# An encoder trunk on one core: a second bias tile requested with the first, two PSUM banks for transposed probabilities, and sums of weight halves formed one split ahead

## The chip, the core and the metric

The kernel runs on one core of one Trainium2 chip. A core has five engines that run side by side, each strictly in the order of its own instruction list, and that wait for each other through semaphores: PE (TensorE, matrix products; PEld is its loading of weights), DVE (VectorE), ACT (ScalarE), POOL (GpSimd) and SP, which here only issues DMAs. [...] The metric is the device time of one execution in microseconds (us). Three runs of the kernel before took 2218.95, 2216.13 and 2218.43 us; the median is 2218.43 us.

## The reference

One inference step of a two-layer encoder trunk for 1024 prompt frames and 32 sample frames, all in float32. Layer 0 is an mLSTM mixer and a SwiGLU feed-forward block, layer 1 a sliding-window attention with 16 heads and a feed-forward block. Cut to what the change touches:

```python
def swiglu(x, w_gu, w_down):
    g, u = jnp.split(x @ w_gu, 2, axis=-1)
    return (jax.nn.silu(g) * u) @ w_down

def sink_attention(q, k, v, sinks, bias):
    s = jnp.einsum('bcqhgd,bckhd->bchgqk', q, k).astype(F32) * (HEAD_DIM ** -0.5) + bias
    sk = sinks.astype(F32).reshape(N_KV_HEADS, GROUP)[:, :, None, None]
    mx = jnp.maximum(jnp.max(s, -1, keepdims=True), sk)
    p = jnp.exp(s - mx)
    p = p / (jnp.sum(p, -1, keepdims=True) + jnp.exp(sk - mx))
    return jnp.einsum('bchgqk,bckhd->bcqhgd', p.astype(v.dtype), v)
```

## The kernel before

**Products.** Every float32 operand is split into a high part and a rest, and each product is three matmuls (L368 to L370: high by high, high by rest, rest by high). A weight comes from memory as a raw tile `wr` (L162, issued by SP), ACT copies its high part to `wh` (L208), and POOL, for some weights DVE, subtracts to get the rest `wl` (L210). One call of `_next` is one such split of one factor. Four raw tiles and five pairs of `wh` and `wl` rotate. A split is written into the program when a factor's last matmul has been written (`done`, L234), up to four factors ahead of its use.

**The up projection of the feed-forward block** runs over 22 tiles of hidden features in each layer. The first two are computed plainly; the other 20 take a fast 2 by 2 scheme with seven products in place of eight. A pair of raw tiles a and b (halves a1, a2, b1, b2) gives seven factors in the order a1, a2, b2, s2, s1, s3, s4. The last four are sums and differences, which DVE forms inside the raw tiles (`_source`: L176, L179, L180, L182): s1 = b1 + b2, s2 = s1 - a1, s3 = a1 - b1, s4 = a2 - s2. Each of these DVE instructions is written right before the ACT copy that reads it, or one or two copies before. The 24 matmuls of one factor take about 2.9 us, one tile about 20.4 us. Bank group A holds the sums that ACT copies out (L1362, L1372, L1379, and L1390 with the silu) before PE adds the next factor on top; group B holds products that DVE adds (L1367, L1375, L1382, L1383). Beside it, `stage` writes activations of earlier tiles to memory for the down projection: ACT (L1288), DVE or POOL (L1289), then a DMA (`hs_t`, `hs_x`). The down projection has pairs of the same kind.

**Attention** (from L1569) runs as a pipeline of five stages over pairs (j, b) of a two-head group and a block of 128 frames: `scores` (PE into two banks `psS`, then DVE adds the bias and takes the extreme, L1725), `soft` (ACT exponent L1737, DVE reciprocal L1741, POOL scaling L1743), `turn` (PE transposes the probabilities into bank `T`, L1763; ACT L1766 and DVE L1767 split them), `values` (PE into one of two banks `O`, L1778 and L1779) and `place` (L1787, L1789). A generator yields after each stage, and the stages are so written in between the matmuls of the query projections (`q_group`) and later of the first quarter of the output projection (L1218); the result of each projection lies in a rotating bank `d` until ACT and DVE have read it (L1623 and L1624, or L1221). `dense_psum(3)` gives `d` three banks here; `psS` has two, `O` two and `T` one, eight in all. The order on each engine is fixed when the program is built.

**The bias** of a head group is a tile `bt` (256 KB) with a smaller `sb` for the sample; two of each rotate. `load_bias` (L1649) has SP issue both DMAs and POOL fill the last column with the sinks. The first is requested at L1659, ahead of the attention's projections; each later one is requested when the first `scores` of the group before it is written (L1712).

## Time and profile before

| what | us |
|---|---|
| median of three runs | 2218.43 |
| the profiled execution: its own time | 2219.82 |
| the profiled execution: span from first to last instruction | 2218.0 |
| PE busy in the span | 2178.0 (98%) |
| DVE busy | 1468.7 (66%) |
| POOL busy | 1020.5 (46%) |
| ACT busy | 1002.6 (45%) |

Times within the execution are counted from the first instruction. Layer 0's fast up tiles run from about 521 to 930 us, its down projection to about 1168, attention from there to about 1430, and layer 1's feed-forward block to the end. A row of the timeline gives start, length, engine, source line, instruction, tile written and tiles read; a bracket at its end gives how long the engine stood idle before it and what ended that. A row of waits gives the waiting instruction, what released it, the total in us, the number of waits and the longest.

### The profile page before, as it was taken

What the parts mean: (1) busy time and instruction counts of PE and PEld (TensorE: products, weight loads), DVE (VectorE), ACT (ScalarE), POOL (GpSimd) and SP (SyncE); (2) the same over time, 40 slices, a digit from 0 to 9 for tenths busy, and PEclk for the clock granted to TensorE, in tenths of its full rate; (3) what the DMA queues carried; (4) which work ended last, traced back from release to release, by engine and by line L of the source; (5) the groups of instructions that cost most, each with busy time, mean ns of one, the idle gap of its engine ahead of it and who ended that gap; (6) DMA issues with size and microseconds to landing.
All of it is one profiled execution on the core that took longest, in us unless ns stands there. A gap on an engine that the chain in (4) does not pass through costs nothing.

```text
span 2218.0 us, 44293 instructions
## 1 busy us (share of the span) xinstructions
PE 2178.0 (98%) x17086; PEld 2149.8 (97%) x17086; DVE 1468.7 (66%) x2848; ACT 1002.6 (45%) x2259; POOL 1020.5 (46%) x982
## 2 busy tenths in 40 slices
PE   9999999999999999999998999999999999999997
PEld 9999999999999999999998999899999999999997
DVE  4465677787666665566667678888576666466657
ACT  4443455464344444321245778756444444422125
POOL 2544210004666566544525776600576666554441
PEclk9999999999999999999999999999999999999999
DMA  5221212212443343797515333521244434397712
GB/s 169 78 62 57 57 39 86 89 39 80 153 155 136 137 155 136 248 333 230 175 57 173 108 100 97 155 63 39 103 162 163 135 138 155 129 343 258 243 59 79
DMA packets 174500, 298.10 MB, mean 134 GB/s; under 512 B 18065, under 2 KB 130761, under 8 KB 174289
## 3 DMA queue, kind: packets, MB, share of 16 engines
q1 hardware_dynamic: 169936, 290.94, 39.9%
q10 hardware_dynamic: 4352, 4.33, 0.6%
q8 instruction: 135, 2.21, 0.4%
q14 instruction: 77, 0.62, 0.1%
HBM read 201.80 MB, written 82.94 MB: 128 GB/s over the span
## 4 chain that ended last, share of the span: by engine, by line
PE 61%; DVE 5%; ACT 3%; DMA 2%; issue 2%; POOL 2%; SPq 0%; POOLq 0%; DVEq 0%; ACTq 0%
PE A L368 9%; PE A L370 9%; PE A L369 9%; PE B L368 6%; PE B L369 6%; PE B L370 6%; PE d L368 4%; PE d L370 4%; PE d L369 4%; PE T L1763 1%; POOL s L1743 1%; DMA hs_x<-z 1%; DMA sx<-hs_t 1%; ACT act L471 1%; PE O L1778 1%
## 5 line engine op out<-in xcount | busy, mean ns | idle before, releaser
L210 POOL TENSOR_TENSOR wl_s<-wr,wh_s 128x512 fp32r<-128x512 f32 x224 | 316.6, 1433 | 262.6 <-ACT wh_s L208 187.6
L210 POOL TENSOR_TENSOR wl_a<-wr,wh_a 128x512 fp32r<-128x512 f32 x112 | 168.7, 1513 | 386.7 <-ACT wh_a L208 264.5
L368 PE MATMUL d<-sx,wh 128*128 128x264 f32 (+2 forms) x1068 | 341.3, 320 | 2.1 <-ACT wh L208 1.6
L370 PE MATMUL d<-sx,wl 128*128 128x264 f32 (+2 forms) x1068 | 325.7, 305 | 2.8 <-POOL wl L210 2.8
L369 PE MATMUL d<-sx,wh 128*128 128x264 f32 (+2 forms) x1068 | 324.8, 304 | 0.4 <-DVE sx L399 0.4
L208 ACT CAST wh_s<-wr 128x512 fp32r<-128x512 f32 x224 | 136.0, 619 | 323.4 <-DVE wr L180 295.6
L368 PE MATMUL A<-sx,wh_s 128*128 128x264 f32 x896 | 254.8, 284 | 1.8 <-ACT z L1372 1.8
L369 PE MATMUL A<-sx,wh_s 128*128 128x264 f32 x896 | 254.2, 284 | 0.0
L370 PE MATMUL A<-sx,wl_s 128*128 128x264 f32 x896 | 254.0, 284 | 0.0
L368 PEld LDWEIGHTS d<-sx,wh 128*128 128x128 f32 x1068 | 201.9, 189 | 5.8 <-ACT wh L208 2.3
L370 PEld LDWEIGHTS d<-sx,wl 128*128 128x128 f32 x1068 | 201.3, 189 | 4.2 <-POOL wl L210 3.9
L369 PEld LDWEIGHTS d<-sx,wh 128*128 128x128 f32 x1068 | 202.1, 189 | 1.5 <-DVE sx L399 0.7
L368 PE MATMUL d<-sx,ex 128*128 128x264 f32 x624 | 180.5, 289 | 0.1
L369 PE MATMUL d<-sx,ex 128*128 128x264 f32 x624 | 177.2, 284 | 0.0
L370 PE MATMUL d<-sx,ex 128*128 128x264 f32 x624 | 176.9, 284 | 0.0
L368 PEld LDWEIGHTS A<-sx,wh_s 128*128 128x128 f32 x896 | 168.4, 188 | 2.4 <-ACT z L1372 2.2
L370 PEld LDWEIGHTS A<-sx,wl_s 128*128 128x128 f32 x896 | 168.8, 188 | 0.0
L369 PEld LDWEIGHTS A<-sx,wh_s 128*128 128x128 f32 x896 | 168.4, 188 | 0.0
L1289 POOL TENSOR_TENSOR z<-z 128x528 fp32r<-128x528 f32 x76 | 104.8, 1378 | 113.4 <-ACT z L1288 106.8
L210 POOL TENSOR_TENSOR wl<-wr,wh 128x512 fp32r<-128x512 f32 (+2 forms) x81 | 104.1, 1293 | 93.1 <-ACT wh L208 89.3
L1743 POOL TENSOR_SCALAR s<-s,st 128x256 f32<-128x256 f32 (+1 forms) x144 | 123.1, 867 | 47.9 <-DVE st L1741 32.0
L1288 ACT CAST z<-z 128x528 fp32r<-128x528 f32 x136 | 86.1, 633 | 94.2 <-DVE z L1301 39.1
(348 smaller groups left out, 7307.3 us busy)
## 6 DMA issues: line engine op xcount, KB each, us to landing
wr<-in_gu SPq DMA_DIRECT2D x92, 512.0 KB
hs_x<-z SPq DMA_DIRECT2D x72, 528.0 KB
hs_t<-z SPq DMA_DIRECT2D x64, 528.0 KB
sx<-hs_x SPq DMA_DIRECT2D x112, 264.0 KB
sx<-hs_t SPq DMA_DIRECT2D x64, 264.0 KB
ex<-hs_t SPq DMA_DIRECT2D x64, 264.0 KB
wr<-in_dn SPq DMA_DIRECT2D x32, 512.0 KB
ex<-hs_x SPq DMA_DIRECT2D x32, 264.0 KB
```

The source lines that it names most:

```text
L208: self.nc.scalar.copy(hi, r)
L210: eng.tensor_sub(lo, r, hi.bitcast(F32))
L368: nc.tensor.matmul(out, ah, bh, start=start and k == 0, stop=False, **kw)
L369: nc.tensor.matmul(out, ah, bl, start=False, stop=False, **kw)
L370: nc.tensor.matmul(out, al, bh, start=False, stop=stop and k == last, **kw)
L471: nc.scalar.activation(z, z, AF.Identity, scale=gk, bias=bk)
L1288: nc.scalar.copy(hi.bitcast(F32R), buf(s))
L1289: eng.tensor_sub(lo.bitcast(F32R), buf(s), hi)
L1743: nc.gpsimd.tensor_scalar_mul(p[:R, h, lo:256], p[:R, h, lo:256], st[:R, 2, h : h + 1])
L1763: nc.tensor.transpose(pt[:nk, i, h, :R], p[:R, h, c : c + nk], ident[:R, :R])
L1778: nc.tensor.matmul(po[:, :, :R], v, s["hi"][:nk, i, :, :R], start=(i == 0), stop=False)
```

## The change

Four edits in three places:

- `load_bias` is called for head group 1 right behind group 0, with its two DMAs only; the POOL copies of the sinks stay where they were (`end_bias`, called at the first `scores`). Later bias tiles are requested as before.
- `T` gets two banks, and `d` gets two in place of three: `psS` two, `O` two, eight in all.
- For the 40 pairs of the up projection (`W.early`) the sums are put elsewhere: s2 in a's first half, s3 in b's second half, s1 and s4 where they were. The number of DVE instructions stays four to a pair.
- For the same pairs the sums are written one split ahead: when a split has been written, `prepare` writes the DVE work of the next factor behind it. Pairs of the down projection go through `_in_place`, which is the old code.

```diff
@@ -141,6 +141,7 @@
         self.jobs, self.last = [], {}
         self.wait, self.ahead, self.pause = 0.0, False, FEED_W
         self.depth = RAW - 1
+        self.made, self.early = set(), set()
         self.spare, self.spared = None, set()
         u = 0
         while u < len(units):
@@ -168,6 +169,17 @@
         n = self.units[u].shape[-1] // 2
         if f in (0, 1):
             return self.raw[u][:, f * n : (f + 1) * n]
+        if u not in self.early:
+            return self._in_place(u, f, n)
+        self.prepare(u, f)
+        a, b = self.raw[u], self.raw[u + 1]
+        return {
+            "a1": a[:, :n], "a2": a[:, n : 2 * n], "b2": b[:, n : 2 * n],
+            "s1": b[:, :n], "s2": a[:, :n], "s3": b[:, n : 2 * n], "s4": a[:, n : 2 * n],
+        }[f]
+
+    def _in_place(self, u, f, n):
+
         sub, add = self.nc.vector.tensor_sub, self.nc.vector.tensor_add
         a, b = self.raw[u], self.raw[u + 1]
         a1, a2, b1, b2 = a[:, :n], a[:, n : 2 * n], b[:, :n], b[:, n : 2 * n]
@@ -181,6 +193,23 @@
         elif f == "s1":
             sub(a2, a2, b2)
         return {"a1": a1, "a2": a2, "b2": b2, "s1": b1, "s2": b2, "s3": a1, "s4": a2}[f]
+
+    def prepare(self, u, f):
+
+        if (u, f) in self.made or f not in ("s2", "s3", "s4"):
+            return
+        self.made.add((u, f))
+        sub, add = self.nc.vector.tensor_sub, self.nc.vector.tensor_add
+        n = self.units[u].shape[-1] // 2
+        a, b = self.raw[u], self.raw[u + 1]
+        a1, a2, b1, b2 = a[:, :n], a[:, n : 2 * n], b[:, :n], b[:, n : 2 * n]
+        if f == "s2":
+            add(b1, b1, b2)
+            sub(a1, b1, a1)
+        elif f == "s3":
+            sub(b2, b2, a1)
+        else:
+            sub(a2, a2, a1)
 
     def _next(self):
         if self.njob == len(self.jobs):
@@ -216,6 +245,10 @@
                 del self.raw[u + 1]
                 u += 1
             self.load_to(u + self.depth)
+        if self.njob < len(self.jobs):
+            u, f = self.jobs[self.njob]
+            if u in self.early and u in self.raw and u + 1 in self.raw:
+                self.prepare(u, f)
         return True
 
     def split_to(self, i):
@@ -321,6 +354,7 @@
     on_vector.update((u, f) for u in U_O + U_OUT_A[0] + U_OUT_B[1] for f in range(2))
     on_vector.update((u, f) for u in U_Q[:1] for f in range(2))
     W = Weights(nc, base, units, pairs, on_vector)
+    W.early = {up[i] for up in U_UP for i in range(FIRST, FT)}
     wv.feed = W.feed
 
 
@@ -1646,17 +1680,25 @@
 
     B = {}
 
-    def load_bias(j):
+    def load_bias(j, sinks=True):
+        if j in B:
+            return end_bias(j)
         at, bufs = (pb2, 1) if j == 5 else (pb, 2)
         bt = new(at, "bt", [P, 2, 257], bufs=bufs)
         sb = new(at, "sb", [DEC, 2, 161], bufs=bufs)
         nc.sync.dma_start(bt[:, :, 0:256], A["bias"][:, 2 * j : 2 * j + 2, :])
         nc.sync.dma_start(sb[:, :, 0:160], A["bias"][:DEC, 2 * j : 2 * j + 2, 0:160])
+        B[j] = (bt, sb)
+        if sinks:
+            end_bias(j)
+
+    def end_bias(j):
+        bt, sb = B[j]
         nc.gpsimd.tensor_copy(bt[:, :, 256], nsink[:, 2 * j : 2 * j + 2])
         nc.gpsimd.tensor_copy(sb[:, :, 160], nsink[:DEC, 2 * j : 2 * j + 2])
-        B[j] = (bt, sb)
 
     load_bias(0)
+    load_bias(1, False)
     def keys_values(g):
         if g == 2:
             k_part(ck[:], SEQ, P)
@@ -1676,7 +1718,7 @@
     lx.close()
     lx.zx.close()
     psx[0].close()
-    dense_psum(3)
+    dense_psum(2)
     psb0 = eb.enter_context(pool("psb0", PSUM))
     psS = [psb0.tile([P, 512], F32, name=f"psS{h}") for h in range(2)]
     for h in range(2):
@@ -1709,6 +1751,8 @@
             if b == 0 or b == 3 and j < 4:
                 ast["visit"] += 1
                 if ast["visit"] < len(visits):
+                    if ast["visit"] > 1:
+                        B.pop(visits[ast["visit"]], None)
                     load_bias(visits[ast["visit"]])
             s = S[j, b] = {}
             lo, k0 = window(b)
@@ -1754,7 +1798,7 @@
             _, t0, R, g, off = CH[b]
             s = S[j, b]
             p = s["p"]
-            pt = new(psb, "T", [P, 2, 2, P])
+            pt = new(psb, "T", [P, 2, 2, P], bufs=2)
             hi = s["hi"] = new(pb2, "hi", [P, 2, 2, P], F32R, bufs=2)
             lo = s["lo"] = new(pb2, "lo", [P, 2, 2, P], F32R, bufs=2)
             kts = key_tiles(b)
```

**On DVE, where layer 0's third pair is prepared** (about 560 to 572 us). `wr_6618` and `wr_6620` are its raw tiles a and b; `z` holds gate and up values, `B` is the bank group. Before:

```order
L1313 TENSOR_TENSOR z_4631<-z_4631 128x528
L176 TENSOR_TENSOR wr_6618<-wr_6618,wr_6620 128x512
L1382 TENSOR_TENSOR z_4631<-z_4631,B_6917 128x528
L1383 TENSOR_TENSOR z_4631<-z_4631,B_6917 128x528
L1384 TENSOR_TENSOR z_4631<-z_4631 128x528
L179 TENSOR_TENSOR wr_6620<-wr_6620 128x512
L180 TENSOR_TENSOR wr_6620<-wr_6620,wr_6618 128x512
L1397 TENSOR_TENSOR z_4631<-z_4631 128x528
L1289 TENSOR_TENSOR z_4631<-z_4631 128x528
L182 TENSOR_TENSOR wr_6618<-wr_6618,wr_6620 128x512
L1300 TENSOR_TENSOR z_4631<-z_4631 128x528
L1301 TENSOR_TENSOR z_4631<-z_4631 128x528
```

The same place in the changed kernel (L207 and L208 make s1 and s2, L210 s3, L212 s4; L1416 to L1418 are the old L1382 to L1384, L1431 is L1397, L1323 is L1289, L1334 and L1335 are L1300 and L1301):

```order
L1347 TENSOR_TENSOR z_4631<-z_4631 128x528
L207 TENSOR_TENSOR wr_6620<-wr_6620 128x512
L208 TENSOR_TENSOR wr_6618<-wr_6620,wr_6618 128x512
L1416 TENSOR_TENSOR z_4631<-z_4631,B_6917 128x528
L1417 TENSOR_TENSOR z_4631<-z_4631,B_6917 128x528
L1418 TENSOR_TENSOR z_4631<-z_4631 128x528
L1431 TENSOR_TENSOR z_4631<-z_4631 128x528
L1323 TENSOR_TENSOR z_4631<-z_4631 128x528
L210 TENSOR_TENSOR wr_6620<-wr_6620,wr_6618 128x512
L1334 TENSOR_TENSOR z_4631<-z_4631 128x528
L1335 TENSOR_TENSOR z_4631<-z_4631 128x528
L212 TENSOR_TENSOR wr_6618<-wr_6618 128x512
```

The two instructions that s2 needs stand ahead of the three that empty bank group B, no longer behind them; s3 and s4 stand later than before, both ahead of the next reading of B (L1367, now L1401), which is the row behind either piece. PE's, ACT's and POOL's lists hold the same instructions in the same order as before.

**On SP, at the start of attention** (the tile numbers 13949 and 13950 are group 0's bias). Before:

```order
L1639 DMA cv_13946<-in_cache_v 128x128
L1653 DMA bt_13949<-in_bias 128x2x256
L1654 DMA sb_13950<-in_bias 32x2x160
L162 DMA wr_13997<-in_wkv 128x1024
L1589 DMA KH_13940<-KH_13939 64x384
```

In the changed kernel:

```order
L1673 DMA cv_13946<-in_cache_v 128x128
L1689 DMA bt_13949<-in_bias 128x2x256
L1690 DMA sb_13950<-in_bias 32x2x160
L1689 DMA bt_13955<-in_bias 128x2x256
L1690 DMA sb_13956<-in_bias 32x2x160
L163 DMA wr_14001<-in_wkv 128x1024
L1623 DMA KH_13940<-KH_13939 64x384
```

Group 1's two DMAs, which stood 28 rows further down behind a weight load (`wr` from `in_wqb`), now stand ahead of the first weight load of attention. Nothing else moves on SP.

## The prediction

> **What bounds the kernel now.** I read the busy times by stage first, then PE's waits, then the timeline around the longest of them. The first view gives, for stretches of the span, the length and the busy time of PE, PEld, DVE, ACT and POOL, the granted PE clock, the DMA share and GB/s.

> ```profile
> 600.00:700.00 100.00, 100.00 (x825) 100.00 (x825) 65.13 (x68) 42.31 (x77) 63.51 (x45) 1.00 0.41 144
> 1200.00:1300.00 100.00, 95.08 (x661) 90.78 (x662) 66.27 (x265) 70.56 (x221) 76.05 (x93) 0.97 0.49 133
> 1300.00:1390.00 90.00, 87.06 (x647) 83.96 (x646) 72.83 (x286) 72.28 (x228) 63.88 (x80) 1.00 0.34 92
> 1390.00:1415.00 25.00, 23.76 (x193) 22.64 (x194) 20.59 (x71) 21.17 (x61) 23.61 (x24) 1.00 0.33 102
> 1415.00:1430.00 15.00, 11.42 (x90) 10.46 (x89) 11.08 (x38) 9.03 (x28) 9.27 (x9) 1.00 0.56 167
> ```

> In the steady up projection (600 to 700) PE is busy all the time: whatever the other engines save there is worth nothing. In attention, the other four rows, PE stands idle 4.9, 2.9, 1.2 and 3.6 us. PE's list is the same before and after, so the change can gain only what PE waits, and a lower clock that comes of it. These waits of PE (waiting, released by, us in total, times, longest) are the ones the edits touch:

> ```profile
> PE T L1763 <- DVE lo L1767: 4.0, 4, 1.5
> PE T L1763 <- POOL s L1743: 2.3, 5, 0.7
> PE psS L1719 <- DVE st L1725: 2.0, 2, 1.8
> PE A L368 <- ACT z L1372: 1.8, 2, 1.3
> PE A L370 <- POOL wl_s L210: 0.5, 2, 0.2
> PE A L368 <- ACT z L1362: 0.2, 1, 0.2
> ```

> Transposes wait for the one T bank, scores for bias, and up products for bank group A and late splits.

> **Bias: 1.8 us of waiting and 1.7 of half clock.** SP's issues, then DVE, PE and three windows:

> ```profile
> 1169.38 0.42 SPq L1653 DMA_DIRECT2D bt<-in_bias  x1
> 1175.80 0.34 SPq L162 DMA_DIRECT2D wr<-in_wkv  x1
> 1209.38 1.38 SPq L1653 DMA_DIRECT2D bt<-in_bias  x1
> 1214.83 0.29 DVE L1725 CUSTOM_DVE_ANT_0 s<-psS,bt 128x129 f32<-128x129 f32 x1 [3.34 <-DMA bt<-in_bias]
> 1215.19 0.39 PE L1719 MATMUL psS<-KH,Q 128*128 128x256 f32 x1 [1.82 <-DVE st L1725]
> 1212.70:1216.10 3.40, 1.58 (x11) 1.26 (x10) 1.13 (x6) 0.91 (x6) 0.96 (x3) 1.00 0.86 256
> 1216.15:1219.55 3.40, 3.40 (x17) 3.30 (x15) 2.70 (x11) 2.27 (x8) 1.18 (x2) 0.50 0.31 80
> 1229.81:1233.20 3.39, 3.39 (x15) 3.37 (x16) 1.86 (x9) 1.43 (x6) 3.08 (x3) 0.50 0.66 229
> ```

> Group 1's bias is asked for at 1209.38 and DVE stands 3.34 us until it lands. Behind DVE's L1725 is queued everything else that DVE owes attention, and PE waits 1.82 us for the score bank. Moved to group 0's place, the request is out near 1170. Its two issues (0.42 us and about as much for the small tile) fit before the weight load at 1175.80, so no load is delayed, and what stood behind the old request leaves SP at least 1.4 us sooner. The 5.4 us from issue to DVE's start (1214.83 less 1209.38) then have 40 us of cover; if SP were held up until 1206, the old wait would be back. What is late next is DVE's own work: it is idle from 1211.49 (1214.83 less 3.34), so L1725's two short passes free the score bank before PE arrives at 1213.37 (1215.19 less 1.82). **Term: -1.8.**

> The clock row shows the second price: PE was idle for over half of 1212.70 to 1216.10, and the next 3.4 us are granted 0.50. Half of 3.4 us, 1.7, is lost there. **Term: -1.7**, bounds 0 (the clock drops anyway, for a later gap) and -3.4 (the second stretch, at 1229.81, goes too, since all that leads to it shifts). [...]

> **A second T bank: -2.1 us.** The stalls, the DVE read that frees T before the second of them, and POOL:

> ```profile
> 1313.72 0.63 PE L1763 MATMUL T<-ident,s 128*128 128x128 f32 x4 [0.64 <-DVE lo L1767]
> 1355.13 0.41 PE L1763 MATMUL T<-ident,s 128*128 128x128 f32 x2 [1.05 <-DVE st L1741]
> 1354.29 0.69 DVE L1767 TENSOR_TENSOR lo<-T,hi 128x512 fp32r<-128x512 f32 x1
> 1379.16 0.63 PE L1763 MATMUL T<-ident,s 128*128 128x128 f32 x4 [0.93 <-DVE lo L1767]
> 1376.84 1.83 POOL L1743 TENSOR_SCALAR s<-s,st 128x256 f32<-128x256 f32 x2 [1.42 <-DVE st L1741]
> 1421.31 0.63 PE L1763 MATMUL T<-ident,s 128*128 128x128 f32 x4 [1.46 <-DVE lo L1767]
> 1418.69 1.82 POOL L1743 TENSOR_SCALAR s<-s,st 128x256 f32<-128x256 f32 x2 [1.74 <-DVE st L1741]
> 1420.48 2.74 POOL L210 TENSOR_TENSOR wl<-wr,wh 128x512 fp32r<-128x512 f32 x2
> 1423.20 1.65 POOL L1743 TENSOR_SCALAR s<-s,st 32x160 f32<-32x160 f32 x2
> 1424.91 0.30 PE L1763 MATMUL T<-ident,s 32*128 32x32 f32 x3 [0.42 <-POOL s L1743]
> ```

> The stall at 1355.13 is laid to L1741, but the read of T ends at 1354.98, 0.15 us before, the same lag as at 1313.72 and 1421.31; it is T's too. With two banks a transpose still needs its own probabilities. At 1313.72 and 1355.13 they are long there: 0.64 and 1.05 go whole. At 1379.16 PE is idle from 1378.23 and POOL ends at 1378.67: only 0.4 goes. Behind 1390 POOL is busy 23.61 us of 25, so it sets the pace: what PE saves at 1421.31 it meets again at 1424.91, since POOL runs its scalings and splits from 1418.69 to 1424.85 without a pause, started by DVE and not by PE. I count nothing there. **Term: 0.64 + 1.05 + 0.4 = -2.1**; bounds 0 (all of it met again in POOL) and -5.0 (the 4.0 of the first waits' row and 1.05).

> The price of that bank is d's third. In the timeline of the 28 results that attention's pool d holds, this is the tightest place; DVE empties one bank, and PE begins the result after next:

> ```profile
> 1426.70 0.42 DVE L1221 SCALAR_TENSOR_TENSOR act<-act,d 128x264 f32<-128x264 f32 x1
> 1429.66 0.29 PE L368 MATMUL d<-sx,wh 128*128 128x264 f32 x1
> ```

> With two banks the second has to wait for the first, and it comes 2.5 us later anyway (1429.66 less 1427.12). The cover is the projection between the two; **cost 0**. If a result were read more than 2.5 us later than now, PE would wait for the excess.

> **Up pairs: -2.5 us.**

> ```profile
> 561.34 0.68 DVE L176 TENSOR_TENSOR wr<-wr,wr 128x512 f32<-128x512 f32 x1
> 564.58 0.69 DVE L180 TENSOR_TENSOR wr<-wr,wr 128x512 f32<-128x512 f32 x1
> 565.36 0.62 ACT L208 CAST wh_s<-wr 128x512 fp32r<-128x512 f32 x1 [6.64 <-DVE wr L180]
> 567.84 1.79 DVE L1289 TENSOR_TENSOR z<-z 128x528 fp32r<-128x528 f32 x1
> 575.20 0.59 ACT L1372 COPY z<-A 128x528 f32<-128x528 f32 x1
> 575.84 0.39 PE L368 MATMUL A<-sx,wh_s 128*128 128x264 f32 x1 [1.34 <-ACT z L1372]
> 1607.78 0.39 PE L368 MATMUL A<-sx,wh_s 128*128 128x264 f32 x1 [0.43 <-ACT z L1372]
> L176 DVE TENSOR_TENSOR wr<-wr,wr 128x512 f32<-128x512 f32 x56 | 71.2, 1271 | 0.0
> L180 DVE TENSOR_TENSOR wr<-wr,wr 128x512 f32<-128x512 f32 x56 | 38.8, 693 | 6.2 <-DVE wr L179 0.5
> ```

> ACT stands 6.64 us behind one copy until L180 is through; behind that copy are ACT's silu and staging copy, then DVE's L1289, a DMA, a further staging copy and L1372, for which PE waits 1.34 us. Now s2 is made where s3 was, from 561.34: two instructions of 0.68 end near 562.7, not at 565.27, 2.6 us sooner. POOL's split then runs beside DVE's next sums; in the group rows such an instruction takes 1271 ns in the place beside POOL's splits, and 693 where POOL waits. One that is stretched as far as L1289 here (1.79) costs 1.1 of the 2.6; 1.5 are left, more than 1.34. So I count 1.34, and 0.43 at 1607.78, which has the same chain. The first pair's late splits (0.5 and 0.2 of the waits' rows) go with the earlier s2. **Term: 1.34 + 0.43 + 0.7 = -2.5**; bounds 0 (the chain hangs on the DMA, not on L180) and 0.2 more for PE's restarts. In the other 35 or so tiles nothing is gained.

> **Sum.** 1.8 + 1.7 + 2.1 + 2.5 = 8.1. The profiled execution took 2219.8 with a span of 2218.0; less 8.1 that is 2211.7. It lay 1.4 above the median of 2218.43, and the median less 8.1 is 2210.3. Since three runs lie 2.8 apart, and a run without the half clock has 1.7 less to win, I stay near the upper: **2211.5**.

> **Rivals.**

> *Only the bias counts.* POOL gives back the T term and the up chain hangs on DMAs: 1.8 + 1.7, so 2218.4 to 2219.8 less 3.5, about **2215.6**. For it: POOL's 23.61 of 25 us. Against it: the T stalls at 1313 and 1355 lie where POOL is busy 71%.

> *DVE falls behind POOL (slower).* s2's two sums move into the time of POOL's splits, and a further sum (s3) now stands ahead of the DVE read that ACT's L1372 follows. If all three are stretched from 0.69 to 1.79, that is 2 x 1.1 + 1.8 = 4.0 us; less the 2.6 of advance DVE comes 1.4 late. The point from which it decides: PE waits once L1372 comes later than now by more than its slack, which at 575.84 is used up. In every second of the 40 tiles that is 20 x 1.4 = 28, less the 5.6 of the other terms: **2241**. Against it: PE's unbroken 100.00 of 100.00 in the steady stage, where DVE is busy 65% and no copy is that close. [...]

> *Two d banks are too few (slower).* If DVE came so late that each of the eight output projections after 1385 had to wait 4 us more than its 2.5 us of margin, that would be 32, less 8: **2242**. Nothing in the change adds DVE work there.

> *The bias request doesn't go early.* If SP holds it behind a weight load, only T and up remain: 4.6 us, **2214**. SP's new list and the pause before 1175.80 speak against it.

> *More goes.* Both half-clock stretches and the 1.46 at 1421 vanish: 8.1 + 1.7 + 1.5, **2208** or a little less.

> **How the numbers follow.** Forecast 0.60, only the bias 0.19, DVE behind POOL 0.07, d banks 0.03, request late 0.03, more 0.08. The forecast's own range is 2208.5 to 2214. With the "only the bias" case and the larger gain the range is 2207.0 to 2217.5; outside are the two slower cases and the tails, under 2 in 10. A measurement of this kernel can tell about 0.2% from no change, 4.4 us: below 2214.0 is faster. That is the forecast, the larger gain and a share of the late request: 0.69. Within 0.2% is "only the bias" and the rest of the late request: 0.22. Slower 0.09.

> **What would show it.** DVE's wait for the bias DMA and PE's 1.82 us are gone, and no clock of 0.50 follows at that place. PE's waits for L1767 fall from 4.0 us to near nothing, and those for POOL's L1743 rise by about half of that at most. No first matmul of a projection waits for L1624 or L1221. PE's waits for L1372 and L1362 are gone and ACT no longer stands behind the sum of s2. I am wrong if PE's waits on group A or on `wl_s` appear in the steady up stage, if a bank d is waited for, or if the waits go and the span stays: then POOL or the clock gave them back.

## The result, and the profile after

The changed kernel takes 2213.55 us (median of 18 runs, 2211.42 to 2216.26), the kernel before in the same rounds 2218.32 us (18 runs, 2215.07 to 2220.73). The ratio is 0.998, with a 95% interval from 0.9974 to 0.9987: 4.8 us, or 0.2%, faster. The forecast was 2211.5, with a range from 2207.0 to 2217.5. The profiled execution has a span of 2211.6 us in place of 2218.0. Two runs in a slow state, one of e1 below (2346.22 us) and one of the kernel before beside e11 and e12 (3544.53 us), are left out of all medians and ratios.

The first view is again that of busy times by stage: the stretch, its length, the busy time of PE, PEld, DVE, ACT and POOL, the granted clock, the DMA share and GB/s, now of the changed kernel.

```profile
600.00:700.00 100.00, 100.00 (x825) 100.00 (x824) 62.13 (x68) 43.07 (x77) 56.96 (x45) 1.00 0.41 145
1200.00:1300.00 100.00, 97.70 (x694) 93.83 (x694) 68.41 (x277) 71.72 (x228) 76.58 (x97) 0.98 0.46 123
1300.00:1390.00 90.00, 89.19 (x668) 86.03 (x667) 74.85 (x293) 74.86 (x235) 66.67 (x80) 1.00 0.37 100
1390.00:1415.00 25.00, 22.20 (x177) 20.34 (x176) 19.69 (x66) 19.25 (x58) 22.67 (x24) 1.00 0.35 114
1415.00:1430.00 15.00, 13.12 (x82) 12.62 (x81) 9.50 (x26) 8.35 (x20) 4.02 (x4) 0.77 0.53 157
```

PE's idle time from 1200 to 1300 falls from 4.9 to 2.3 us, from 1300 to 1390 from 2.9 to 0.8. From 1390 to 1415 it rises from 1.2 to 2.8, and the mean clock of the last stretch is 0.77, where it was 1.00. The second view is PE's waits in the changed kernel (waiting, released by, total in us, times, longest):

```profile
PE T L1807 <- POOL s L1787: 5.3, 11, 1.5
PE d L402 <- ACT wh L237: 2.3, 1, 2.3
PE O L1736 <- DVE ql L1658: 0.3, 1, 0.3
PE psS L1763 <- DVE st L1769: 0.2, 1, 0.2
```

The transposes no longer wait for T's reader (4.0 us under `lo` before, and the 1.05 at 1355.13), but for POOL's scaling 5.3 us where it was 2.3. The scores' 2.0 us are 0.2. The waits on group A for L1372, L1362 and the late splits are gone. New in this form is one pause of 2.3 us for ACT's split of a query weight, at 1195.9, where the kernel before waited 1.6 in two pieces. Two further profiles of the changed kernel (e8 and e12 below) have 1.6 and 1.8 in two pieces again, so it isn't there in every execution.

**A ledger.** Both traces hold 17086 matmul records in the same order, so each can be set beside its counterpart. The table gives what each stretch of the kernel before gained (-) or lost (+), in us, in the changed kernel, in e8 and e12, and in the parts tried alone.

```
stretch of before   changed    e8      e12   e1 bias  e2 banks  e3 up  e4 one T  e11 no banks
   1 -  500          -0.58   -0.55   -0.07   +1.04   -0.68   -0.76   -0.62   +0.06
 500 -  650  up      -2.24   -2.24   -2.24   -0.03   -0.02   -2.24   -2.24   -2.24
 650 - 1190          -0.09   +1.25   -0.03   -0.10   -0.05   +0.25   +1.13   +0.51
1190 - 1212          +2.71   +1.47   -0.11   +0.43   +1.41   +0.78   +3.08   +0.64
1212 - 1220  bias    -3.66   -3.66   -3.66   -3.67   -2.14   -2.52   -3.67   -3.66
1220 - 1240          -1.58   -0.02   -0.01   +0.01   +0.02   -0.01   -1.57   -0.03
1300 - 1390  T       -2.04   -2.04   -2.02   -0.03   -2.08   -0.07   -0.07   -0.03
1390 - 1421  T       -0.38   -0.38   -0.42    0.00   -0.42   +0.12   -0.02   -0.04
1421 - 1430  T       +3.78   +0.80   +3.49   +0.12   +3.66   +0.07    0.00   +0.12
1500 - 1650  up      -1.74   -1.69   -1.76   -0.37   -0.07   -1.70   -1.70   -1.76
whole trace          -6.40   -7.21   -6.85   -2.90   -0.41   -6.25   -6.33   -6.93
```

The stretches that the table leaves out add up to 0.7 us at most. The edge at 1421 cuts through PE's stall before 1421.31, so the two rows beside it are to be read as one sum. In this table the rows marked with a part repeat within 0.1 us wherever that part is in the kernel, but for 1421 to 1430; the first row and the stretches from 650 to 1212 differ by up to 3.2 us between profiles that share the code there. Three things stand out: the up part gains 4.0 us, not 2.5; the T part gains its 2.0 us before 1390 and gives back more behind it in all columns with two T banks but e8; and at 1190 to 1212 something is lost that no edit names.

### The profile page after: what moved, and what is told of

The parts are those of the page before. It is cut to its first block, busy times and chain, and to the rows that moved or that the text cites. A ratio compares the mean times of both kernels' runs of the same rounds, so it can differ in the third digit from the quotient of the medians.

```text
span 2211.6 us, 44311 instructions
## 1 busy us (share of the span) xinstructions
PE 2179.2 (99%) x17086; PEld 2152.7 (97%) x17086; DVE 1451.7 (66%) x2848; ACT 1007.8 (46%) x2259; POOL 991.2 (45%) x982
## 4 chain that ended last, share of the span: by engine, by line
PE 86%; DVE 7%; ACT 4%; issue 1%; DMA 1%; POOL 1%; SPq 0%; DVEq 0%; ACTq 0%; POOLq 0%
PE A L402 10%; PE A L404 10%; PE A L403 10%; PE d L402 10%; PE d L404 9%; PE d L403 9%; PE B L402 7%; PE B L403 7%; PE B L404 7%; PE T L1807 1%; ACT act L505 1%; PE O L1822 1%; PE T L955 1%; PE O L1823 1%; PE H L951 1%
## 5 line engine op out<-in xcount | busy, mean ns | idle before, releaser
L239 POOL TENSOR_TENSOR wl_s<-wr,wh_s 128x512 fp32r<-128x512 f32 x224 | 304.1, 1366 | 237.5 <-ACT wh_s L237 168.4
L239 POOL TENSOR_TENSOR wl_a<-wr,wh_a 128x512 fp32r<-128x512 f32 x112 | 153.5, 1373 | 412.5 <-ACT wh_a L237 287.3
L1323 POOL TENSOR_TENSOR z<-z 128x528 fp32r<-128x528 f32 x76 | 103.2, 1358 | 126.3 <-ACT z L1322 117.1
L402 PE MATMUL A<-ex,wh_s 128*128 128x264 f32 x448 | 127.5, 285 | 0.0
```

The costliest lines, as they stand in the source:

```text
L239: eng.tensor_sub(lo, r, hi.bitcast(F32))
L402: nc.tensor.matmul(out, ah, bh, start=start and k == 0, stop=False, **kw)
L1323: eng.tensor_sub(lo.bitcast(F32R), buf(s), hi)
```

## The experiments

All kernels compute what the reference computes. Each was timed beside the kernel before on the same chip; the ratio is to that.

| kernel | median us (runs) | ratio, 95% interval |
|---|---|---|
| e1_bias: early bias alone | 2215.55 (10) | 0.9991 (0.9982 to 1.0) |
| e2_banks: T two, d two alone | 2218.41 (11) | 1.0006 (0.9997 to 1.0014) |
| e3_up: up sums alone | 2213.38 (11) | 0.998 (0.9972 to 0.9989) |
| e4_d2: changed, T one bank | 2213.20 (11) | 0.998 (0.9971 to 0.9989) |
| e5_nolead: changed, sums not ahead | 2223.26 (9) | 1.0026 (1.0016 to 1.0036) |
| e6_fill: changed, filler transposes | 2211.34 (8) | 0.9972 (0.9962 to 0.9982) |
| e7_scale: changed, nine scalings on DVE | 2209.81 (5) | 0.9968 (0.9955 to 0.998) |
| e8_again: changed, one run | 2212.62 (1) | |
| e9_lead: changed, sums ahead in the old places | 2212.58 (11) | 0.9979 (0.9971 to 0.9988) |
| e10_onebank: e7 with T one, d three | 2210.44 (5) | 0.9966 (0.9952 to 0.9979) |
| e11_threed: changed, T one, d three | 2211.79 (10) | 0.9969 (0.996 to 0.9979) |
| e12_after: changed, beside e11 | 2213.88 (11) | 0.9983 (0.9974 to 0.9992) |

### The parts one by one

`e1_bias` is the kernel before with only this:

```diff
     load_bias(0)
+    load_bias(1, False)
```

> The kernel before with the early bias request alone: one T bank, three d banks, sums of the up pairs as before. Theory (three separate shares that add up): PE's wait of 1.82 us for the score bank and DVE's 3.34 us for the bias are gone; the span falls by 1.8 plus up to 1.7 of half clock, so 2 to 3.5 us below the kernel before, ratio 0.9984 to 0.9991. Rival (the wait is only passed on): PE reaches the next shortage sooner, the waits for the first query weights near 1195 or the later ones grow by as much, ratio 0.9997 to 1.0003. Rival (the clock decides): the wait is gone, but a half-clock stretch of 3.4 us or more stands elsewhere in attention, gain under 1 us in this profile while the median of many runs still falls by 2.

Measured: 2215.55 against 2217.26 for the kernel before, 1.7 us, where the interval of the ratio reaches 1.0. The ledger shows the wait gone (-3.67 from 1212 to 1220) and nothing passed on, so the first rival falls. The last one fits in part: the half clock of 1216.15 is gone, but one stands at 1200.50. But the two kernels that keep the late request, e2 and e3, gain 2.1 and 2.5 us there too. Their rows, of PE and DVE in e3 and of PE in e2:

```profile
1211.92 0.29 DVE L1768 CUSTOM_DVE_ANT_0 s<-psS,bt 128x129 f32<-128x129 f32 x1 [2.41 <-DMA bt<-in_bias]
1212.28 0.39 PE L1762 MATMUL psS<-KH,Q 128*128 128x256 f32 x1 [0.87 <-DVE st L1768]
```

```profile
1215.26 0.39 PE L1762 MATMUL psS<-KH,Q 128*128 128x256 f32 x1 [1.22 <-DVE st L1768]
```

There the same late bias costs PE 0.87 and 1.22 us, not 1.82, and no half clock follows. Against these two the early request is worth 3.66 less 2.14 to 2.52, that is 1.1 to 1.5 us; the 1.7 of the time agrees within its interval.

`e2_banks`:

```diff
-    dense_psum(3)
+    dense_psum(2)
...
-            pt = new(psb, "T", [P, 2, 2, P])
+            pt = new(psb, "T", [P, 2, 2, P], bufs=2)
```

> The kernel before with two T banks and two d banks alone. Theory: the stalls of transposes behind DVE's read of T at 1313.7 and 1355.1 go (1.7 us), 0.4 of the one at 1379.2 goes, the others come back as waits for POOL's scaling; 2.1 us in all, ratio 0.9990. Rival (POOL gives all of it back): waits of T for lo fall to zero, waits of T for s rise by as much, ratio 0.9997 to 1.0003. Rival (the lost d bank costs): waits of a projection's first matmul for L1624 or L1221 appear, ratio above 1.0003.

Measured: 1.0006 (0.9997 to 1.0014), so no gain, and the median is 1.2 us above. The waits of e2:

```profile
PE T L1806 <- POOL s L1786: 5.3, 11, 1.5
PE O L1735 <- DVE ql L1658: 0.6, 1, 0.6
```

The waits for `lo` are gone, those for POOL have risen by 3.0. The ledger keeps 2.08 of it before 1390; behind, 3.24 are lost (-0.42 and +3.66). No `d` bank is waited for by a projection, but a new wait stands at the start of attention: the first transpose into an `O` bank waits for L1658, DVE's reading of a query projection. It is in all nine profiles of kernels with two `d` banks (0.35 to 1.66 us), and in none with three; of those, the kernel before and e10 wait near there for another thing, VR (0.64 and 0.92 us). Record by record, this transpose, at 1200.42 in the kernel before, comes 0.75 to 2.07 us later in the nine against the one ahead of it, and 0.00 to 0.20 in the four others with three banks. Where a slow clock of 3.41 us stands near 1200, the kernels with two `d` banks lose 1.41 to 1.88 us from 1190 to 1212 (e2, e5, e7, e8), those with three 0.43 to 0.78 (e1, e3, e11); without one, e12 and e10 lose no more than 0.24, with two banks or three. So `d`'s third bank was worth about 1 us in most of these profiles, at a place that none of the three expectations names. That the `O` bank lies where a `d` bank was is argued from the code and wasn't tried.

`e3_up` has the diff's `prepare` and `W.early`, and neither the bias edit nor the banks.

> The kernel before with the new places and the lead of the up pairs' sums alone. Theory: PE's waits on group A at 575.8 and 1607.8 and for the first pairs' late splits go, 2.5 us as predicted and up to 3.9 us by the excess that the changed kernel no longer shows between 500 and 650 and between 1550 and 1650; ratio 0.9982 to 0.9989. Rival (the chain hangs on the staging copies and DMAs): ACT no longer stands behind the sums, but PE still waits for L1372, ratio 0.9996 to 1.0002. Attention is written as before; its waits are those of the kernel before within run-to-run differences.

Measured: 2213.38 against 2217.26, 3.9 us, and 2.24 and 1.70 in the two stretches of the ledger. The theory holds, at its upper end.

`e4_d2` leaves a bank empty: T one, `d` two, all else as changed.

> The changed kernel with T back to one bank while d keeps two (one of the eight banks stays empty). Theory (T's second bank is worth 2 us, d's third nothing): 2 us slower than the changed kernel, so a ratio to the kernel before of about 0.9987, with T's waits for lo back at 3 to 5 us and no wait of a projection for L1624 or L1221. Rival (T's bank is worth nothing since POOL gives it back): the ratio of the changed kernel, 0.998. Rival (d's third bank had been worth something): waits for a d bank appear, and this kernel is slower than the changed one by more than T's waits explain.

Measured: 0.998, the changed kernel's ratio. The first rival holds in the time: the T bank is worth nothing, though the clock takes it back more than POOL does, as is shown below. In the ledger its 2.0 us before 1390 are missing, and the loss behind 1421 is missing as well. This kernel has the largest wait for a `d` bank's reader near 1200 (1.66 us).

### What of the up part does it

`e5_nolead` keeps the new places, without the lead:

```diff
-            if u in self.early and u in self.raw and u + 1 in self.raw:
+            if False:
                 self.prepare(u, f)
```

> The changed kernel with the sums of the up pairs in their new places but written where they are needed, not one split ahead. Theory (the new place alone frees s2 from the split of b2; the lead adds little): the up stages keep most of the 4.0 us that the changed kernel gains there (2.24 between 500 and 650, 1.75 between 1500 and 1650), at least 3; the time is that of the changed kernel within 1 us, ratio 0.998 to 0.9985. Rival (the lead does it): ACT stands behind the sums again, the stall near 575 is back and the time is 3 to 4 us above the changed kernel, ratio 0.9995 or more.

Measured: 2223.26 us, 5.3 above the kernel before and some 10 above the changed one: the theory falls, and the rival was too mild. In the ledger it loses 2.67 us from 650 to 1190, of which 2.25 lie before 935, and 2.73 from 1650 to 1900; from 650 to 935 and from 1650 to 1900 every other kernel stands within 0.01 us of the kernel before. The stalls at 575.84 and 1607.78 stay away in e5 too; its own begin at 594.76 and 1629.10. PE's and ACT's waits in e5:

```profile
PE A L402 <- ACT z L1406: 3.5, 14, 0.6
ACT wh_s L237 <- DVE wr L208: 188.4, 40, 6.0
ACT wh_s L237 <- DVE wr L212: 62.4, 36, 2.9
ACT wh_s L237 <- DVE wr L210: 39.3, 24, 2.2
```

From there on PE waits in every second tile, 14 times in all, for L1406, the staging copy (L1372 of the kernel before). The timeline of one such place, DVE then ACT:

```profile
633.46 0.71 DVE L1347 TENSOR_TENSOR z<-z 128x528 f32<-128x528 f32 x1 [2.65 <-POOL z L1323]
634.09 0.69 DVE L212 TENSOR_TENSOR wr<-wr 128x512 f32<-128x512 f32 x1
634.86 0.62 ACT L237 CAST wh_s<-wr 128x512 fp32r<-128x512 f32 x1 [2.85 <-DVE wr L212]
635.39 0.59 ACT L1406 COPY z<-A 128x528 f32<-128x528 f32 x1
```

DVE stands 2.65 us for a staging multiplication of POOL; the sum for s4 (L212) is queued behind it, ACT's copy behind that, and behind the copy the staging copy that PE needs. In the old places s3 was formed before b2's copy and s4 before s1's, ahead of their own; in the new ones each sum comes right before its own copy. So the new places alone make two of the sums later.

`e9_lead` is the opposite: the old places, with the lead.

```diff
-            "s1": b[:, :n], "s2": a[:, :n], "s3": b[:, n : 2 * n], "s4": a[:, n : 2 * n],
+            "s1": b[:, :n], "s2": b[:, n : 2 * n], "s3": a[:, :n], "s4": a[:, n : 2 * n],
...
+        if f == "b2":
+            sub(a1, a1, b1)
+        elif f == "s2":
             add(b1, b1, b2)
-            sub(a1, b1, a1)
...
```

> The changed kernel with the up pairs' sums in the old places (s2 in b's second half, s3 in a's first) and yet written one split ahead. Theory (the lead and the place only help together: in the old place s2 overwrites b2, so a sum written one split ahead makes DVE wait for POOL's split of b2, with DVE's readouts for PE queued behind it): DVE shows waits for POOL's wl in the up stages, PE's waits on group A come back, the up stages keep at most half of the 4.0 us; ratio 0.999 or more. Rival (the lead alone does it, since s3 and s4 no longer stand before their copies and s2's wait is short): the gain of the changed kernel stays, ratio 0.998. Rival (it is worse still): PE waits in every second tile as in the kernel without the lead, ratio above 1.001.

Measured: 0.9979 (0.9971 to 0.9988), the whole gain, with -2.24 and -1.76 in the two up stretches. The theory falls, the first rival holds. In e9 the wait for POOL's split of b2 is there, and costs nothing:

```profile
DVE wr L210 <- POOL wl_b L239: 79.3, 32, 3.7
ACT wh_s L237 <- DVE wr L210: 104.4, 36, 4.3
```

DVE waits 79.3 us for POOL and ACT 104.4 for DVE, and PE waits for neither in the up stages. The lead is the edit that counts.

### Where the T bank's gain goes

In the changed kernel POOL and PE stand like this before the last transposes:

```profile
1411.69 1.83 POOL L1787 TENSOR_SCALAR s<-s,st 128x256 f32<-128x256 f32 x2 [1.74 <-PE O L1822]
1413.48 2.75 POOL L239 TENSOR_TENSOR wl<-wr,wh 128x512 fp32r<-128x512 f32 x2
1416.21 1.53 POOL L1787 TENSOR_SCALAR s<-s,st 32x160 f32<-32x160 f32 x2
```

```profile
1417.14 0.24 PE L1807 MATMUL T<-ident,s 32*128 32x32 f32 x1 [1.46 <-POOL s L1787]
1417.80 0.30 PE L1807 MATMUL T<-ident,s 32*128 32x32 f32 x3 [0.41 <-POOL s L1787]
```

Of the kernel before, the prediction shows the rows at 1421.31 (1.46 us of waiting for `lo`) and 1424.91 (0.42); between them stands this one:

```profile
1424.25 0.24 PE L1763 MATMUL T<-ident,s 32*128 32x32 f32 x1 [0.75 <-POOL s L1743]
```

The 1.46 us at the first of these transposes have become 0.34 and 0.58, now for POOL's scaling. PE so comes sooner to the next one, where its wait has grown from 0.75 to 1.46, right ahead of the 0.41 that was there already. In this trace the half clock begins at 1197.23 and at 1419.10 and lasts 6.83 us each time, twice the 3.41 us that each of the kernel before's stretches took. Windows of 3.40 us around the two places read:

```profile
1193.80:1197.20 3.40, 0.62 (x2) 0.30 (x2) 2.79 (x7) 3.40 (x7) 1.25 (x1) 1.00 1.03 310
1197.20:1200.60 3.40, 2.75 (x8) 2.25 (x9) 2.31 (x7) 2.97 (x8) 3.40 (x4) 0.51 0.68 220
1415.70:1419.10 3.40, 1.54 (x13) 1.38 (x13) 1.76 (x6) 1.10 (x6) 2.05 (x3) 1.00 0.78 213
1419.10:1422.50 3.40, 3.40 (x17) 3.27 (x16) 2.68 (x6) 1.79 (x6) 1.27 (x1) 0.50 0.55 137
```

A window in which PE is busy 0.62 of 3.40 us is followed here by one at 0.51, one of 1.54 by one at 0.50. From 1418 to 1430 of this trace PE is busy without a break, and of the projection's matmuls one starts every 0.22 us in the half clock and every 0.12 behind it, so nearly half of the 6.83 us is lost: the ledger has +3.0 us between 1425 and 1430.

`e8_again` is the changed kernel once more.

> The changed kernel once more, for a second profile. Theory (the half clock near 1197 and near 1419 follows the pauses of PE at 1195.9 and 1417.1 in every execution): both stretches are there again, each 3.4 or 6.8 us long. Rival (the window runs free of the program): at least one of them is missing or begins at a place that differs by more than 1 us against the instructions.

Measured: near 1200 a stretch of 3.41 us in place of 6.83, one more at 1226.99, and behind 1418 none. The theory falls; the half clock moves against the program. Its windows at the last transposes:

```profile
1414.70:1418.10 3.40, 2.11 (x16) 1.90 (x16) 3.31 (x9) 3.05 (x10) 3.40 (x4) 1.00 0.20 45
1418.10:1421.50 3.40, 2.28 (x19) 2.12 (x19) 1.64 (x7) 1.41 (x5) 1.36 (x3) 1.00 0.84 242
```

The same pauses (1.47 and 0.42 us) fall here into two windows, PE is busy 2.11 and 2.28 us of them, neither is followed by a clock of 0.50, and the stretch from 1421 to 1430 loses 0.80 and not 3.78. Of the six profiles with two T banks and POOL's load unchanged, five have the slow clock there (6.83 us in the changed kernel, e2, e5 and e12, 3.41 in e9). Of the five with one T bank, three have 3.41 us of it, and from 1390 to 1430 they lose 0.2 us at most: it ends before PE's waits for POOL, which become shorter by as much. The windows of e1:

```profile
1415.60:1419.00 3.40, 1.95 (x15) 1.68 (x14) 2.59 (x10) 3.35 (x11) 2.73 (x3) 0.99 0.40 144
1419.00:1422.40 3.40, 3.40 (x17) 3.40 (x16) 2.51 (x8) 1.66 (x6) 3.17 (x4) 0.50 0.51 154
```

`e6_fill` keeps PE busy in those pauses:

```diff
+            few = {(7, 6): (2, 0), (7, 7): (2, 3), (7, 8): (8, 2)}.get((j, b), (0, 0))
             for i, (c, nk, _) in enumerate(kts):
                 for h in range(2):
+                    for _ in range(few[h] if i == 0 else 0):
+                        nc.tensor.transpose(pt[:, 1, 1, :], ident[:], ident[:])
```

> The changed kernel with 17 additional transposes of the identity (0.16 us each) into the T bank ahead of or between the last three transposes of probabilities, where PE stands for POOL's scaling; they are overwritten. Theory (the second T bank's gain of 2.1 us before 1390 is returned behind 1410 by a half clock of 6.8 us that follows the PE pause of 1.9 us at 1417): with PE kept busy no clock of 0.50 follows, 3 us less than the changed kernel, ratio 0.9965 to 0.997. Rival (the pace of POOL takes it back, the clock does not matter): the fillers change nothing, or cost up to 0.5 us where they outlast the pauses; ratio 0.998.

Measured: 2211.34 us, ratio 0.9972 (0.9962 to 0.9982): 2.2 us below the changed kernel's median, though their intervals overlap, and between the theory's 0.9965 to 0.997 and the rival's 0.998. PE's rows and the windows of e6:

```profile
1417.13 1.04 PE L1809 MATMUL T<-ident 128*128 128x128 f32 x8
1418.76 0.24 PE L1810 MATMUL T<-ident,s 32*128 32x32 f32 x1 [0.59 <-POOL s L1787]
```

```profile
1415.40:1418.80 3.40, 2.81 (x25) 2.58 (x23) 3.19 (x9) 2.29 (x8) 3.40 (x4) 1.00 0.39 106
1418.80:1422.20 3.40, 3.35 (x25) 2.94 (x26) 1.56 (x5) 2.13 (x6) 1.36 (x2) 1.00 0.73 218
```

No slow clock follows, and from 1421 to 1430 the ledger loses 0.82 where the changed kernel loses 3.78. That is also what e8 shows without fillers, so one profile would not settle it. Each run's mean granted clock is on record too: as a mean of the runs it is 0.9970 in e6 and 0.9956 in the changed kernel, and a difference of 0.0014 over 2211 us makes 6.2 us more at half clock. Profile, clock and median together speak for the clock.

`e7_scale` relieves POOL:

```diff
             for h in range(2):
-                nc.gpsimd.tensor_scalar_mul(p[:R, h, lo:256], p[:R, h, lo:256], st[:R, 2, h : h + 1])
+                eng = nc.vector if h == 1 and (j == 6 and b > 5 or j == 7 and b > 2) else nc.gpsimd
+                eng.tensor_scalar_mul(p[:R, h, lo:256], p[:R, h, lo:256], st[:R, 2, h : h + 1])
```

> The changed kernel with one of the two scalings of the last nine attention pairs on DVE in place of POOL (9 x 0.91 us off POOL, 9 x about 0.4 onto DVE). Theory (POOL sets the pace behind 1390 and so returned what the T bank had won): waits of transposes for s fall from 5.3 us to under 2.5, the half clock near 1419 goes, 3 to 5 us less than the changed kernel, ratio 0.996 to 0.997. Rival (DVE is as full as POOL there): the waits move to DVE, T then waits for DVE's scaling or lo, and the time stays, ratio 0.998 or more. Rival (only the clock matters): the waits fall but a half clock stands elsewhere, gain under 1 us.

Measured: 2209.81 us, ratio 0.9968 (0.9955 to 0.998), the lowest median of the study. The stage behind 1390, and the transposes' waits, in e7:

```profile
1390.00:1415.00 25.00, 22.64 (x181) 20.90 (x179) 22.80 (x76) 20.59 (x60) 17.73 (x17) 1.00 0.38 119
```

```profile
PE T L1808 <- POOL s L1788: 3.2, 5, 1.1
```

POOL is busy 17.73 in place of 22.67 us, DVE 22.80 in place of 19.69; the waits fall by 2.1 (to 3.2, not under 2.5 as expected), and no slow clock stands behind 1410. From 1390 to 1430 the ledger gains 1.5 (-1.77, +0.20 and +0.03), where the changed kernel loses 3.4 (-0.38 and +3.78).

`e10_onebank` is e7 with one T bank and three `d` banks.

> The kernel with nine scalings on DVE (e7_scale), but with one T bank and three d banks. Theory (with POOL relieved, the second T bank keeps its 2.0 us between 1300 and 1390, and more behind): 2 to 4 us above e7_scale, ratio to the kernel before about 0.998, waits of T for lo back at 3 us or more. Rival (the relief alone makes the gain and the bank is worth nothing): the ratio of e7_scale, 0.9968.

Measured: 0.9966 (0.9952 to 0.9979), no different from e7 in time, as the rival has it, though the waits for `lo` are back (5.2 us). In the ledger e7 holds 2.05 us from 1300 to 1390 that e10 does not have, and both gain 1.5 behind; but e10 lost only 0.24 from 1190 to 1212, and e7 1.88, with 1.02 of waiting for a `d` bank's reader among it. Whether the second bank pays once POOL is relieved stays open: with five runs of each, the clock moves the time by as much.

`e11_threed` takes only the banks back, `e12_after` is the changed kernel in the same rounds.

> The changed kernel without the bank edit: early bias request and new up sums, one T bank, three d banks. Theory (the bank edit gives 2.0 us between 1300 and 1390 and gives it back near 1203, near 1395 and, by a half clock, behind 1417): equal to the changed kernel or up to 2 us faster, ratio 0.997 to 0.998; no wait of a transpose into O for L1658 near 1203 and no costly half clock near 1425. Rival (the bank edit is worth its 2.1 us): 2 us slower than the changed kernel, ratio 0.9988.

> The changed kernel once more beside the one without its bank edit, in the same rounds. Theory: ratio 0.9978 again, at or up to 2 us above the kernel without the bank edit, with a half clock of 3.4 or 6.8 us behind the pause near 1417 in most executions. Rival: 2 us below it.

Measured: 2211.79 (0.996 to 0.9979) without the banks, 2213.88 (0.9974 to 0.9992) with them. The median is 2.1 us lower without. The two intervals, each taken against the kernel before, overlap between 0.9974 and 0.9979; but set directly beside each other, eight of e11's ten runs are faster than the fastest of e12's eleven. The mean granted clock of the runs is 0.9974 without the banks and 0.9953 with them, 9.3 us less at half clock. So the whole bank edit costs about 2 us in these rounds. That e4, which takes back T's bank alone, showed no difference points to `d`'s third bank as a part of this; e4 and e11 were timed on different chips, and the share of each bank wasn't tried in the same rounds. The waits of e11 are back where they were, for `lo` and not for POOL:

```profile
PE T L1807 <- DVE lo L1811: 4.0, 4, 1.4
PE T L1807 <- POOL s L1787: 1.1, 3, 0.6
```

## Why the prediction was right, and where it was not

The forecast, that PE's waits at three places would go and the kernel gain some 0.3%, came out as 0.2%: 4.8 us of the 8.1. PE's waits went at all three places, and no rival came about as a whole, though the T term was given back, as "only the bias counts" had it (there by POOL). That the time, 2213.55, lies inside the forecast's own range of 2208.5 to 2214 is in part luck: one term was too small and the three others too large, and with the up term at its 2.5 the time would have been about 2215.

**Bias, -1.8.** The mechanism was right: the request goes out ahead of the weights, DVE's 3.34 us and PE's 1.82 are gone, and the next three weight requests follow the old ones' order with no delay. The size was that of one execution: in e2 and e3 the wait was 1.22 and 0.87. The early request is worth 1.1 to 1.5 us by the ledger, and 1.7 by the time of e1.

**Half clock after the bias wait, -1.7.** This step failed. The half clock at 1216 isn't there in e2 and e3 either, which keep the late bias: of three profiles with the late request one has it. Its absence in the changed kernel can't be credited to the edit. Nor does the clock come cleanly out of the sum: in the changed kernel's profile 2.71 us are lost from 1190 to 1212, where it lay at 1197.2 for 6.83 us after a pause of 2.35, and 1.58 come back from 1220 to 1240, where the half clock of 1229.81 is missing. In e12, the same program, neither stretch differs by more than 0.11.

**Second T bank, -2.1.** The sum holds: 2.04 us, and 2.02 to 2.11 in every kernel with two T banks but e5 (1.81). Its parts do not, so the agreement is in part luck. The changed kernel gains 0.65 us from 1300 to 1320 and 0.80 from 1320 to 1360 (for 0.64 and 1.05), only 0.08 from 1360 to 1385 (for 0.4, with new waits for POOL at 1371.76 and 1375.26), and 0.52 behind 1385, where a wait for POOL's split at 1388.51 went that the prediction hadn't counted. "I count nothing there", of what lies behind 1390, holds for POOL: -0.38 and +0.77 (1421 to 1425) make +0.4. What failed is that only POOL was asked. PE came sooner to the next transpose, its wait there grew to 1.46 us right ahead of the next pause, and in five profiles of six the clock took 1.5 to 3.0 us for it between 1425 and 1430. The prediction had named this as what would prove it wrong: the waits go, and POOL or the clock gives them back. For this term it did.

**d's third bank, 0.** The margin of 2.5 us held: no projection waits for a `d` bank. Missed was the start of attention, which the 28 results of its own pool do not show: there PE's first transpose into `O` waits 0.35 to 1.66 us for a `d` bank's reader, which costs about 1 us where the slow clock stands there. By the ledger the bank edit as a whole is -2.0 before 1390, that +1 in most profiles, and behind 1390 +3.4 with the slow clock (changed) or +0.4 without it (e8); the 2.1 us between e11 and e12 lie within these bounds.

**Up pairs, -2.5.** The right stalls went, and the five listed by the trace (1.34, 0.43, and 0.24, 0.24 and 0.22 at the first pairs) add up to 2.5. The ledger has 2.24 + 1.74 = 4.0. The rest is what PE loses around each stall beside the idle time. Matmuls of the kernel before around 575:

```profile
574.10 0.28 PE L369 MATMUL B<-ex,wh_b 128*128 128x264 f32 x1
574.22 0.28 PE L370 MATMUL B<-ex,wl_b 128*128 128x264 f32 x1
...
576.07 0.28 PE L369 MATMUL A<-sx,wh_s 128*128 128x264 f32 x1
576.19 0.28 PE L370 MATMUL A<-sx,wl_s 128*128 128x264 f32 x1
```

In a stream one starts every 0.12 us. From 574.22 to the waiting one at 575.84 it is 1.62, and from there to 576.07 another 0.23: 1.85 us for two steps of 0.12, so 1.61 lost, where the bracket shows 1.34. The other four show the same: between the two traces 0.70, 0.51, 0.51 and 0.49 go at stalls of 0.43, 0.24, 0.24 and 0.22. So 0.27 more for each of five stalls is 1.35; the prediction had allowed 0.2 for all of them. One of the five, at 1559.91, is missing in e1 as well, where the up pairs are as before, so 0.4 of the 4.0 may not be the edit's. As to the cause, the prediction didn't say which of the two up edits brings s2 forward; e5's expectation gave it to the new place. Experiments e5 and e9 show that the lead does it, and that the place without the lead, with the bias and bank edits beside it, costs 5 us. The slower rival, "DVE falls behind POOL", put its waits into every second tile; that is the pattern of e5, at 0.16 to 0.64 us each.

**Sum.** 1.7 + 3.9 less 1.2, by the medians of the parts alone, is 4.4; the whole measured 4.8.

## What to carry to other kernels

Work that feeds a queue is worth writing a step ahead of its use, even if it then waits for another engine, as in e9; a new place in memory that merely allows this gained nothing here by itself and made other work later. Before moving a stall out of the way, look at what pause it will land next to, and add up PE's idle time over a few microseconds (here 1.46 and 0.41 us within 3.40), not stall by stall. A gain of 0.1% is better proved by stretches of two traces that repeat across kernels, and a half clock in a single profile belongs to that execution until a second one shows it.
